# State-space gate of a hybrid attention and state-space block: two single passes of 512 columns against one paired pass of 1024 columns behind the state-space part

## The chip, the cores and the metric

The kernel runs on one core of a Trainium2 chip. The metric is device time in microseconds (us), median of several runs; lower is better. Names of engines are those of the profile: PE is TensorE's matmuls and PEld its weight loads, DVE is VectorE, ACT is ScalarE, POOL is GpSimd, and SP is SyncE, which issues nearly all DMAs.

## The reference

One layer: an RMS norm, one wide projection, dilated attention on one branch, a chunked state-space scan on the other, and two sigmoid gates that mix the branches. There are 256 rows (tokens), D is 2048, and the state-space width is 4096 in 8 groups. All data are fp32.

```python
hn = rms_norm(x, norm_w)
proj = hn @ w_in
q, k, v, z_a, z_s, xbc, dt_raw, g_a, g_s = jnp.split(proj, split_points, axis=-1)
...
y = rms_norm(y * jax.nn.silu(z_s), ssm_norm_w)
merged = jax.nn.sigmoid(g_a) * (o_a @ w_attn_branch) + jax.nn.sigmoid(g_s) * (y @ w_ssm_branch)
return x + merged @ w_out
```

The change concerns g_s, the gate of the state-space branch: 2048 columns, in quarters of 512 that the kernel numbers 0 to 3.

## The kernel before

**Products in three parts.** Each fp32 weight is split into a high part (h, an ACT copy, L276) and a low part (l, a DVE subtraction, L277). A product is then three matmuls: high by high, high by low, low by high. The weights come in units of 1024 columns (512 KB). A unit passes through three rings with a slot count each: w (5 slots, the load), h and l (4 slots each).

**Single pass.** `gates` (L588) calls `gemm_b` (L399): 16 steps of the inner dimension, two row blocks, three matmuls of 512 columns each, so 96 matmuls for one quarter of g_s. ACT then writes the tanh of the sums into th_s (L591).

**Paired pass.** `gemm_pair` (L461) makes 1024 columns at once. It walks over quads: two steps of the inner dimension by two row blocks by two column blocks. A plain quad is eight block products of three matmuls, 24 in all, out of two units. A quad listed in `S_QUADS` is done with seven block products (Strassen's scheme in Winograd's form), 21 matmuls. For these it loads wa and a sum of weight blocks wt, part of the fourth block wc, and sums of blocks of the left operand (sx). It makes ha and la from wa, hc and lc from wc (all four in the rings h and l, L550 and L552), then ht and lt from wt, and hu and lu from wa less wt (these in the pool `mul`). Where a (pass, quad) is listed in `presum`, the sum wt has been made ahead by DVE, sent to DRAM (`sum_jobs`, L242) and is loaded back (L525). Eight PSUM banks are used: four accumulators es and four products prods, one set on the tag g and the other on m1 and m2; `swap` says which. `fold` (L577) puts the products together. `room` gives places of their own for wt and wc ("wt", "wc") and for some of the ht and lt ("tl").

**Stages in order.** First come dt and quarters 0 and 1 of g_s; then eight groups of the state-space part, each with projections B, C and four pairs xs, zs (`project`, one bank of tag g each). Quarter 2 of g_s stands ahead of group 4 and quarter 3 behind group 7 (L947). Then follow paired passes for the state-space branch (ssm, L990), for v (L1023), the heads of attention, the gate g_a, the attention branch and the output.

**The tail of a group.** Work that waits for data is put off with `after(ticks, f)`; a tick is one projection or two units. For a group these are `turn` (transposes of xs, L793), four `decays` (L772: a load into acb, ACT operations into gt, a DVE product at the end of every second one), `scan` (L811, 32 small matmuls on PE, which read gt) and two `gather` (L828, DVE and ACT, which write yT). gt, acb, xdt and y1 have one buffer each. `tick(final=True)` (L948) puts out whatever is left.

**Places.** The tail's buffers lie in the pool `ssm` (L685), which closes after L948. The pools `mul` (L951), `xk` (L965) and `xp` (L977) are opened behind it and take the same part of the on-chip memory. Tiles of one tag share its slots. Within an engine, the order of instructions is fixed when the kernel is built: an instruction that comes earlier in the program has priority, one that isn't ready is overtaken, and the splits of units are lifted by 120 places (L274, L547).

The left sums sx of x for quads 2, 4, 5 and 6 are made in the group loop and kept in DRAM (`left_x`, L902); `fetch_left` (L429) brings one back: a POOL cast of one column behind a given unit, then a DMA on SP.

Of the kernel before, what the change touches and what calls it, by code (L numbers as in the profile page):

```python
# [1 line left out]

# [7 lines left out]
F32 = mybir.dt.float32  # L10
F32R = mybir.dt.float32r
# [24 lines left out]
N_ACT_X = 1  # L36
DT_LAG, CB_LAG, TURN_LAG, GT_LAG, Y_LAG, S_LAG, M_LAG = 2, 5, 3, 2, 11, 2, 2
Y_AFTER = 0, 0
GS_BEFORE = {0: (0, 1), 4: (2,)}
A_ORDERS = {0: (0, 1, 2, 4, 3, 6, 5, 7), 2: (0, 2, 1, 4, 3, 5, 6, 7)}  # L40
V_ORDERS = {0: (0, 2, 4, 1, 3, 5, 6, 7), 2: (0, 2, 1, 4, 3, 5, 6, 7)}
G_ORDERS = {c: (0, 2, 1, 4, 3, 5, 6, 7) for c in (0, 2)}
# [3 lines left out]
NEG = -1.0e30  # L46
S_QUADS = {
    ("ssm", 0): (5, 7, 8, 10, 11, 12, 13), ("ssm", 2): (3, 5, 7, 8, 10, 11, 12, 13),
    ("v", 0): (2, 3, 4, 5, 6), ("v", 2): (2, 4, 5, 6), ("ga", 0): (2, 4, 5, 6), ("ga", 2): (2, 4, 5, 6),
    ("attn", 0): (2, 4, 6), ("attn", 2): (2, 4, 5, 6), ("out", 0): (3, 5), ("out", 2): (3, 5),  # L50
}
# [7 lines left out]
SUMS_ATT = [(t, q) for t in [(n, c) for n in ("ga", "attn", "out") for c in (0, 2)] for q in S_QUADS[t]]  # L59
ATT_QUADS = sorted({*S_QUADS[("attn", 0)], *S_QUADS[("attn", 2)]})  # L60
IN_PLACE = {"ssm": [(0, 12), (2, 12)]}
SUMS_SSM = [(t, q) for t in (("ssm", 0), ("ssm", 2), ("v", 0), ("v", 2)) for q in S_QUADS[t] if (t[1], q) not in IN_PLACE.get(t[0], ())]
SUM_UNITS = 2, 9, 16
LEFT_EVERY, ATT_EVERY = 11, 4
SUM_LAG = 3
ROOM_SSM = 2
# [15 lines left out]
def weight_plan():  # L82
    plan = []

    def cols(tag, src, off, n_kt):
        plan.append((tag, "a", src, off, n_kt, P))

    def rows(tag, src, off, n_kt):
        plan.append((tag, "b", src, off, n_kt, 512))

    def pair(tag, src, off, n_kt):
        plan.append((tag, "p", src, off, n_kt, 1024))

    plan.append((("first", 0), "m", "w_in", (OFF_B, OFF_C, OFF_X, OFF_ZS), KT, 512))
    plan.append((("dt", 0), "a", "w_in", OFF_DT, KT, SH))
    for g in range(GROUPS):
        for c in GS_BEFORE.get(g, ()):
            rows(("gs", c), "w_in", OFF_GS + c * 512, KT)
        if g > 0:
            cols(("B", g), "w_in", OFF_B + g * P, KT)  # L100
            cols(("C", g), "w_in", OFF_C + g * P, KT)
        for t in range(max(4 * g, 1), 4 * g + 4):
            cols(("xs", t), "w_in", OFF_X + t * P, KT)
            cols(("zs", t), "w_in", OFF_ZS + t * P, KT)
    rows(("gs", 3), "w_in", OFF_GS + 3 * 512, KT)
    for c in (0, 2):
        pair(("ssm", c), "w_ssm_branch", c * 512, 2 * KT)
    for c in (0, 2):
        pair(("v", c), "w_in", OFF_V + c * 512, KT)
    for h in range(NH):  # L110
        cols(("q", h), "w_in", OFF_Q + h * P, KT)
        cols(("k", h), "w_in", OFF_K + h * P, KT)
        cols(("za", h), "w_in", OFF_ZA + h * P, KT)
    for c in (0, 2):
        pair(("ga", c), "w_in", OFF_GA + c * 512, KT)
    for c in (0, 2):
        pair(("attn", c), "w_attn_branch", c * 512, KT)
    for c in (0, 2):
        pair(("out", c), "w_out", c * 512, KT)
    return plan  # L120
# [76 lines left out]
def hybrid_block(ctx: ExitStack, tc: tile.TileContext, wall, xt, x, pk_d, cst_d, fw_d, out):  # L197
# [26 lines left out]
    def bank(tag, bufs, name):  # L224
        return ps.tile([P, 512], F32, name=name, tag=tag, bufs=bufs)
# [70 lines left out]
    def two_kts(t, q):  # L296
        t, q = (t[q // 4], q % 4) if isinstance(t, list) else (t, q)
        return t[:, 2 * q : 2 * q + 2, :]
# [130 lines left out]
    def fetch_left(kept, pool, bufs, key, x, spare, u):  # L429
        def get(behind):  # L430
            sx = new_sx(pool, bufs, spare, f"{key[0]}{key[1]}")
            gp.tensor_copy(sx[:, 0, 0, 0:1], behind)
            nc.sync.dma_start(sx.bitcast(F32), lefts[key])
            kept[key[1]] = left_parts(sx, x, spare)

        behind_unit(u, get)
# [151 lines left out]
    def gates(tag, th, src, scales=(0.5, 0.5)):  # L588
        accs = gemm_b(tag, lambda kt: kt_of(src, kt))
        for i in range(2):  # L590
            ac.activation(th[:, i, tag[1] * 512 : tag[1] * 512 + 512], accs[i], AF.Tanh, scale=scales[i])  # L591
# [93 lines left out]
    with tc.tile_pool(name="ssm", bufs=2) as sp:  # L685
# [223 lines left out]
        for g in range(GROUPS):  # L909
# [9 lines left out]
            for t in range(max(4 * g, 1), 4 * g + 4):  # L919
# [24 lines left out]
                zh = ev.tile([P, S], F32, name=f"zh{t}", tag="eh", bufs=2)  # L944
                evac(acc, zh, f"z{t}", scale=0.5)
                half_silu(zh, state["zs"][-1][:, i], f"z{t}")
        gates(("gs", 3), th_s, XT)  # L947
        tick(final=True)  # L948


    mul = ctx.enter_context(tc.tile_pool(name="mul", bufs=1))  # L951

    def scale_gate():
        tot = bank("m1", 2, "tot_y")
        for i in range(2):
            for n in range(2):
                pe.matmul(
                    tot[:, 2 * i : 2 * i + 2], ssq[:, n, i * P : (i + 1) * P], ones[:, 0:2],
                    start=(n == 0), stop=(n == 1),
                )  # L960
        _, hr = rsqrt_rows(tot[:, 0:4:2], INNER, "y")
        for i in range(2):
            ac.activation(th_s[:, i], th_s[:, i], AF.Identity, scale=hr[:, i : i + 1], bias=hr[:, i : i + 1])
# [1 line left out]
    xk = ctx.enter_context(tc.tile_pool(name="xk", bufs=1))  # L965
    sx_of_x = {}

    for n, q in enumerate(SX_X[:1]):
        fetch_left(sx_of_x, xk, 1, ("x", q), two_kts(XT, q), 0, plain_unit(("ssm", 2), 12, Y_ORDERS[2]))
    def room_of(t, n_wt, n_wc):  # L970
        t = t.rearrange("p (n m) -> p n m", m=512)
        return {
            "wt": [t[:, 2 * n : 2 * n + 2].rearrange("p n m -> p (n m)") for n in range(n_wt)],
            "wc": [t[:, 2 * n_wt + n] for n in range(n_wc)],
        }

    with tc.tile_pool(name="xp", bufs=1) as xp:  # L977
        sxs = {}
        ssm_room = room_of(xp.tile([P, ROOM_SSM * 512], F32, name="room_s", tag="room"), 0, ROOM_SSM)

        def left_y(q):
            spare = Y_SPARE[q]
            sx = new_sx(xp, sum(s == spare for s in Y_SPARE.values()), spare, f"y{q}")
            sxs[q] = turn_x(sx, ring(f"sxt_y{q}").rearrange("p (n m) -> p n m", n=2), two_kts(yT, q), spare)

        for q in SX_Y:
            if q in Y_LATE:
                continue
            fetch_left(sxs, xp, sum(s == Y_SPARE[q] for s in Y_SPARE.values()), ("y", q), two_kts(yT, q), Y_SPARE[q], plain_unit(("ssm", 0), Y_ORDERS[0].index(q) - 3 if q in S_QUADS[("ssm", 0)] else 12, Y_ORDERS[0]))
        for c in (0, 2):  # L990
            es, prods = gemm_pair(
                ("ssm", c), lambda kt: kt_of(yT, kt), 2 * KT, sxs, c == 2, {} if c else {2: [scale_gate], **{u: [lambda q=q: left_y(q)] for q, u in Y_LATE.items()}},
                1, Y_ORDERS[c], ssm_room,
            )
            tmp = [mul.tile([P, UNIT], F32, name=f"tmp_{t}{c}", tag=t, bufs=2) for t in ("ht", "lt")]
            dst = [t[:, n * 512 : n * 512 + 512] for t in tmp for n in range(2)]
            fold(prods, dst)
            for d, e, g in zip(dst, es, blocks(th_s, c)):
                ve.tensor_tensor(d, e, d, ALU.add)
                ve.tensor_tensor(g, g, d, ALU.mult)  # L1000
# [15 lines left out]
    with tc.tile_pool(name="vx", bufs=1) as vx:  # L1016
        tl = big.tile([P, 4, UNIT], F32R, name="tl_v", tag="yo0b")
        room["tl"] = [(tl[:, 2 * n], tl[:, 2 * n + 1]) for n in range(2)]
        for n, q in enumerate(SX_V):
            fetch_left(sx_of_x, vx, len(SX_V), ("x", q), two_kts(XT, q), 0, FIRST[("v", 0)])  # L1020
        for n, q in enumerate(SX_X[1:]):
            fetch_left(sx_of_x, xl, len(SX_X) - 1, ("x", q), two_kts(XT, q), 0, FIRST[("v", 0)] + 1 + n)
        for c in (0, 2):  # L1023
            es, prods = gemm_pair(
                ("v", c), lambda kt: XT[:, kt, :], KT, sx_of_x, c == 2, order=V_ORDERS[c], room=room
            )
            dst = blocks(vt, c)
            fold(prods, dst)
            for d, e in zip(dst, es):
                ve.tensor_tensor(d, e, d, ALU.add)  # L1030
    sx_of_o = {}

    with tc.tile_pool(name="att", bufs=2) as ap:
# [55 lines left out]
        for h in range(NH):  # L1089
            q, k = (ap.tile([P, S], F32, name=f"{n}T{h}", tag=f"{n}T", bufs=2) for n in "qk")  # L1090

            for n, d in (("q", q), ("k", k)):
                evac(project((n, h)), d, f"{n}{h}")
            p = ap.tile([P, 384], F32, name=f"p{h}", tag="p", bufs=2)
            pT = ap.tile([P, 384], F32, name=f"pT{h}", tag="pT", bufs=1)
            za = ap.tile([P, S], F32, name=f"za{h}", tag="za", bufs=3)
            after(S_LAG + (6, 4, 2)[max(h - 13, 0)], lambda a=(h, pT, za): mix(*a))
            after(S_LAG + (3 if h < 15 else 1), lambda a=(h, p, pT): turn_p(*a))
            after(S_LAG + (h == 0), lambda a=(h, q, k, p): scores(*a))
            zh = ev.tile([P, S], F32, name=f"zah{h}", tag="eh", bufs=2)  # L1100
            evac(project(("za", h)), zh, f"za{h}", scale=0.5)
            half_silu(zh, za, f"za{h}")
# [169 lines left out]
```

## Time and profile before

| what | value |
|---|---|
| median of 3 runs | 1385.69 us (1385.48 to 1386.45) |
| profiled execution, span from first to last instruction | 1383.8 us |
| mean granted TensorE clock | 0.998 |
| group loop up to the last projection | about 80 to 558 us |
| last single gate pass (quarter 3) | 558 to 581 us |
| scan of group 7 on PE | 581 to 584 us |
| paired passes of the state-space branch | 584 to 748 us |
| DMA moved | 345 MB, mean 249 GB/s |

The span is that of one profiled execution, 1.9 us below the median of the runs. Times in the views are counted from the start of that span. In the view of windows the columns are: the window, its length, busy time of PE, PEld, DVE, ACT and POOL (with the number of instructions), the granted clock, the DMA share and GB/s. In the view of waits a line reads: who waited, for whom, us in total, times, the longest. In the timeline: start, duration, engine, line, operation, what it writes and reads, how many were merged.

### The profile page before, as it was taken

The numbers are of one execution on the slowest core, as the hardware profiler recorded it, in microseconds if no ns is written. First come the engines' busy times: TensorE is split into PE (matmuls) and PEld (weight loads), VectorE is DVE, ScalarE is ACT, GpSimd is POOL, SyncE is SP. The second block draws the span as 40 slices with busy tenths as digits, with TensorE's granted clock in tenths as the row PEclk, the third lists the DMA queues.
The fourth block names the chain that finished last, engine by engine and source line by source line (L and its number), as shares of the span: only waits on it lengthen the run. The fifth ranks groups of instructions, "written<-read, shape, count | busy, mean of one in ns | idle before, by whom it ended". The sixth has DMA issues, their size and how long they took to land.

```text
span 1383.8 us, 20696 instructions
## 1 busy us (share of the span) xinstructions
PE 1373.6 (99%) x7266; PEld 1169.9 (85%) x7266; DVE 1169.5 (85%) x1753; ACT 835.5 (60%) x1306; POOL 142.0 (10%) x226
## 2 busy tenths in 40 slices
PE   9999999999999999999999999999999999999997
PEld 8888888888888888888888888888888888888886
DVE  7898999987799898789889897777877788888897
ACT  7656677675667675766565554544544556655564
POOL 2301111101011100010001001111111000000112
PEclk9999999999999999999999999999999999999999
DMA  9767988868787866668677668888888757865773
GB/s 347 231 187 225 313 254 291 279 224 287 245 266 240 294 212 208 188 224 280 230 259 267 222 209 278 275 275 273 299 288 301 241 161 264 294 222 180 243 273 122
DMA packets 105080, 345.00 MB, mean 249 GB/s; under 512 B 11728, under 2 KB 13712, under 8 KB 104976
## 3 DMA queue, kind: packets, MB, share of 16 engines
q1 hardware_dynamic: 103536, 339.62, 74.0%
q10 hardware_dynamic: 1440, 4.06, 0.8%
q8 instruction: 57, 0.93, 0.3%
q14 instruction: 47, 0.39, 0.1%
HBM read 314.87 MB, written 28.77 MB: 248 GB/s over the span
## 4 chain that ended last, share of the span: by engine, by line
PE 97%; DMA 1%; DVE 1%; ACT 1%; issue 0%; SPq 0%; POOL 0%; POOLq 0%; DVEq 0%; ACTq 0%
PE ps_zs L329 8%; PE ps_xs L329 8%; PE ps_zs L332 4%; PE ps_q L329 4%; PE ps_za L329 4%; PE ps_k L329 4%; PE ps_xs L332 4%; PE ps_ssm L476 3%; PE ps_ssm L477 3%; PE ps_ssm L478 3%; PE ps_q L332 2%; PE ps_k L332 2%; PE ps_za L332 2%; PE ps_gs L414 2%; PE ps_gs L412 2%; PE ps_gs L413 2%
## 5 line engine op out<-in xcount | busy, mean ns | idle before, releaser
L276 ACT ACTIVATE h<-w 128x1024 fp32r<-128x1024 f32 (+1 forms) x398 | 413.9, 1047 | 318.0 <-issue 78.8
L277 DVE TENSOR_TENSOR l<-w,h 128x1024 fp32r<-128x1024 f32 (+1 forms) x398 | 479.4, 1211 | 124.2 <-ACT h L276 121.8
L329 PE MATMUL ps_zs<-XT,h 128*128 128x512 f32 x496 | 176.3, 397 | 0.0
L329 PE MATMUL ps_xs<-XT,h 128*128 128x512 f32 x496 | 175.9, 396 | 0.0
L332 PE MATMUL ps_zs<-XT,l 128*128 128x256 f32 x496 | 139.9, 282 | 0.0
L332 PE MATMUL ps_xs<-XT,l 128*128 128x256 f32 x496 | 139.8, 282 | 0.0
L329 PEld LDWEIGHTS ps_xs<-XT,h 128*128 128x128 f32 x496 | 93.3, 188 | 21.7
L329 PEld LDWEIGHTS ps_zs<-XT,h 128*128 128x128 f32 x496 | 93.4, 188 | 21.2
L332 PEld LDWEIGHTS ps_zs<-XT,l 128*128 128x128 f32 x496 | 93.7, 189 | 1.5 <-issue 0.7
L332 PEld LDWEIGHTS ps_xs<-XT,l 128*128 128x128 f32 x496 | 93.7, 189 | 0.4
L329 PE MATMUL ps_q<-XT,h 128*128 128x512 f32 x256 | 92.5, 405 | 0.2 <-ACT h L276 0.2
L329 PE MATMUL ps_k<-XT,h 128*128 128x512 f32 x256 | 89.9, 395 | 0.0
L329 PE MATMUL ps_za<-XT,h 128*128 128x512 f32 x256 | 89.7, 394 | 0.0
L543 ACT ACTIVATE ha<-wa 128x1024 fp32r<-128x1024 f32 x43 | 45.4, 1055 | 46.4 <-DMA wa<-in_wall 10.9
L332 PE MATMUL ps_q<-XT,l 128*128 128x256 f32 x256 | 71.2, 278 | 0.0
L332 PE MATMUL ps_k<-XT,l 128*128 128x256 f32 x256 | 71.1, 278 | 0.0
L332 PE MATMUL ps_za<-XT,l 128*128 128x256 f32 x256 | 71.1, 278 | 0.0
L544 DVE TENSOR_TENSOR la<-wa,ha 128x1024 fp32r<-128x1024 f32 x43 | 52.5, 1220 | 11.9 <-ACT ha L543 11.8
L782 ACT ACTIVATE gt<-acb,acT 128x128 f32<-128x128 f32 x128 | 44.2, 391 | 23.7 <-DMA acb<-acum_d 21.9
L329 PEld LDWEIGHTS ps_q<-XT,h 128*128 128x128 f32 x256 | 48.2, 188 | 11.5 <-ACT h L276 0.6
L329 PEld LDWEIGHTS ps_za<-XT,h 128*128 128x128 f32 x256 | 48.1, 188 | 11.3
L329 PEld LDWEIGHTS ps_k<-XT,h 128*128 128x128 f32 x256 | 48.1, 188 | 11.2
(688 smaller groups left out, 3325.1 us busy)
## 6 DMA issues: line engine op xcount, KB each, us to landing
w<-in_wall SPq DMA_DIRECT2D x394, 512.0 KB, 4.7
wa<-in_wall SPq DMA_DIRECT2D x43, 512.0 KB, 4.9
th_a<-in_wall SPq DMA_DIRECT2D x19, 512.0 KB, 5.6
sums_at<-in_wall SPq DMA_DIRECT2D x18, 512.0 KB, 4.7
acb<-acum_d SPq DMA_DIRECT2D x32, 256.0 KB, 4.0
t_ssm<-sums_at SPq DMA_DIRECT2D x13, 512.0 KB, 4.1
wt<-t_ssm SPq DMA_DIRECT2D x13, 512.0 KB, 5.4
th_a<-in_wall SPq DMA_DIRECT2D x19, 256.0 KB, 6.0
```

What stands on the lines that cost most here:

```text
L276: ac.activation(h[:, a:b], w[:, a:b], AF.Copy)
L277: ve.tensor_tensor(l[:, a:b], w[:, a:b], h[:, a:b].bitcast(F32), ALU.subtract)
L329: pe.matmul(acc, h[:, kk, :], m, start=(kt == 0), stop=False)
L332: pe.matmul(acc[:, S:], l[:, kk, :], m[:, :S], start=False, stop=(kt == KT - 1))
L412: pe.matmul(accs[i], xh, h[:, kk], start=(kt == 0), stop=False)
L413: pe.matmul(accs[i], xh, l[:, kk], start=False, stop=False)
L476: pe.matmul(acc, xh, h, start=start, stop=False)
L477: pe.matmul(acc, xh, l, start=False, stop=False)
L478: pe.matmul(acc, xl, h, start=False, stop=stop)
L543: ac.activation(h, src, AF.Copy)
L544: ve.tensor_tensor(l, src, h.bitcast(F32), ALU.subtract)
L782: ac.activation(g4[:, n, b], acb[:, j, b // 2 * P : b // 2 * P + P], AF.Relu, scale=-1.0, bias=sc[:, h : h + 1],)
```

## The change

Quarters 2 and 3 of g_s are made in one paired pass, ("gs", 2), which comes behind the closed pool ssm and ahead of the state-space branch. Its order is quads 0, 1, 2, 4, 3, 5, 6, 7, and quads 2, 4, 5 and 6 have seven products. It has a pool of its own, gx: places for two wt and one wc, one pair of ht and lt more, and three sx; the sx of quad 2 goes to xk and is kept for the pass v. Four weight sums are added to those made ahead, and these are now made four times in a group instead of three: 24 of them instead of 18. With one paired pass more in front, the passes ssm and v exchange their sets of banks, the sum of squares tot_y moves from tag m1 to g, and q and k of head 0 go to m1 and m2.

```diff
-GS_BEFORE = {0: (0, 1), 4: (2,)}
+GS_BEFORE = {0: (0, 1)}
+GS_ORDER = (0, 1, 2, 4, 3, 5, 6, 7)
...
+    ("gs", 2): (2, 4, 5, 6),
...
-SUMS_SSM = [(t, q) for t in (("ssm", 0), ("ssm", 2), ("v", 0), ("v", 2)) for q in S_QUADS[t] if (t[1], q) not in IN_PLACE.get(t[0], ())]
-SUM_UNITS = 2, 9, 16
+SUMS_SSM = [(t, q) for t in (("gs", 2), ("ssm", 0), ("ssm", 2), ("v", 0), ("v", 2)) for q in S_QUADS[t] if (t[1], q) not in IN_PLACE.get(t[0], ())]
+SUM_UNITS = 1, 6, 11, 16
...
-    rows(("gs", 3), "w_in", OFF_GS + 3 * 512, KT)
+    pair(("gs", 2), "w_in", OFF_GS + 2 * 512, KT)
...
-        gates(("gs", 3), th_s, XT)
         tick(final=True)
...
-        tot = bank("m1", 2, "tot_y")
+        tot = bank("g", 4, "tot_y")
...
-    for n, q in enumerate(SX_X[:1]):
-        fetch_left(sx_of_x, xk, 1, ("x", q), two_kts(XT, q), 0, plain_unit(("ssm", 2), 12, Y_ORDERS[2]))
...
+    with tc.tile_pool(name="gx", bufs=1) as gx:
+        room = room_of(gx.tile([P, 5 * 512], F32, name="room_g", tag="room"), 2, 1)
+        tl = gx.tile([P, 2, UNIT], F32R, name="tl_g", tag="tl")
+        room["tl"] = [(tl[:, 0], tl[:, 1])]
+        sx_of_g = {}
+        for n, q in enumerate(SX_X):
+            pool, kept = (gx, sx_of_g) if n else (xk, sx_of_x)
+            fetch_left(kept, pool, max(n and len(SX_X) - 1, 1), ("x", q), two_kts(XT, q), 0, FIRST[("gs", 2)] + n)
+        es, prods = gemm_pair(
+            ("gs", 2), lambda kt: XT[:, kt, :], KT, ChainMap(sx_of_g, sx_of_x), False, order=GS_ORDER, room=room
+        )
+        dst = blocks(th_s, 2)
+        fold(prods, dst)
+        for d, e in zip(dst, es):
+            ve.tensor_tensor(d, e, d, ALU.add)
+            ac.activation(d, d, AF.Tanh, scale=0.5)
...
-                ("ssm", c), lambda kt: kt_of(yT, kt), 2 * KT, sxs, c == 2, {} if c else {2: [scale_gate], **{u: [lambda q=q: left_y(q)] for q, u in Y_LATE.items()}},
+                ("ssm", c), lambda kt: kt_of(yT, kt), 2 * KT, sxs, c == 0, {} if c else {2: [scale_gate], **{u: [lambda q=q: left_y(q)] for q, u in Y_LATE.items()}},
...
-                ("v", c), lambda kt: XT[:, kt, :], KT, sx_of_x, c == 2, order=V_ORDERS[c], room=room
+                ("v", c), lambda kt: XT[:, kt, :], KT, sx_of_x, c == 0, order=V_ORDERS[c], room=room
...
-                evac(project((n, h)), d, f"{n}{h}")
+                evac(project((n, h), None if h else {"q": "m1", "k": "m2"}[n]), d, f"{n}{h}")
```

More of the change, by code (lines that the diff above doesn't have):

```diff
@@ L1 @@
+from collections import ChainMap
 from contextlib import ExitStack, nullcontext
```

## The prediction, made before the changed kernel ran

> **What bounds the kernel now.** I read the page first, then who PE waits for, then busy time by stage.
>
> ```profile
> span 1383.8 us, 20696 instructions
> ...
> PE 1373.6 (99%) x7266; PEld 1169.9 (85%) x7266; DVE 1169.5 (85%) x1753; ACT 835.5 (60%) x1306; POOL 142.0 (10%) x226
> ...
> PEclk9999999999999999999999999999999999999999
> ```
> ```profile
> PE ps_q L329 <- ACT h L276: 0.2, 1, 0.2
> ```
> ```profile
> 80.00:293.00 213.00, 213.00 (x1273) 184.41 (x1272) 194.85 (x336) 143.86 (x270) 25.85 (x54) 1.00 0.82 265
> ...
> 316.00:558.00 242.00, 242.00 (x1452) 209.32 (x1451) 207.56 (x337) 159.90 (x299) 22.27 (x48) 1.00 0.76 247
> 558.00:580.70 22.70, 22.70 (x106) 18.72 (x104) 17.78 (x20) 17.32 (x34) 0.00 (x0) 1.00 0.64 196
> ```
>
> TensorE sets the time: it is busy 99% of the span at the full clock, and its one wait after the start is 0.2 us. In the windows (PE, PEld, DVE, ACT, POOL, clock, DMA share, GB/s) PE fills the group loop and also the last gate pass (558 to 580.7). So a matmul taken away is worth its spacing, but only while PE never runs dry; in this kernel any hole in PE is paid in full. The question is whether the pass in its new place can keep PE fed.
>
> **The change: what it removes.** These rows of PE's timeline carry the sum (start, duration):
>
> ```profile
> 549.78 2.82 PE L820 MATMUL yp<-gt,xdt 128*64 128x256 f32 x32
> ...
> 557.93 0.28 PE L332 MATMUL ps_zs<-XT,l 128*128 128x256 f32 x1
> ...
> 558.74 0.39 PE L412 MATMUL ps_gs<-h,XT 128*128 128x512 f32 x1
> ...
> 561.46 0.39 PE L412 MATMUL ps_gs<-h,XT 128*128 128x512 f32 x1
> ...
> 564.18 1.03 PE L801 MATMUL xtp<-cst,xs 128*128 128x128 f32 x8
> 564.97 0.47 PE L412 MATMUL ps_gs<-h,XT 128*128 128x512 f32 x1
> ```
> ```profile
> 580.83 2.82 PE L820 MATMUL yp<-gt,xdt 128*64 128x256 f32 x32
> 583.58 0.50 PE L476 MATMUL ps_ssm<-h,yTa 128*128 128x512 f32 x1
> ```
>
> From 558.74 to 561.46 twelve 512-column matmuls start: 2.72/12 = 0.227 us each. Two single passes are 2 x 96 = 192 of them; the new pass has four plain quads of 24 and four of 21, 180. **Saved: 12 x 0.227 = 2.7 us**, 0.2% of the time.
>
> **What it moves.** The last projection ends at Z (here 558.05, after the 557.93 row; earlier by one gate pass afterwards). Behind Z stands the tail of the last group: decays, transposes, scan, gather. Now that tail lies beside the third gate pass and four plain quads of the ssm pass. Afterwards no gate pass stands there, and only two plain quads come before the first quad of seven products. That quad needs the pools mul, xk and gx, which are opened where the closed pool ssm lay. The waits of SP and ACT from 583 to 600, before:
>
> ```profile
> SPq L526 <- DVE yT L288: 3.8, 1, 3.8
> ```
> ```profile
> ACT htt L543 <- DVE yT L288: 2.0, 1, 2.0
> ```
> ```profile
> 583.70 0.88 DVE L833 SCALAR_TENSOR_TENSOR y<-xs,pk,yp 128x256 f32<-128x256 f32 x2 [0.45 <-PE yp L820]
> ...
> 588.31 1.22 DVE L277 TENSOR_TENSOR l<-w,h 128x1024 fp32r<-128x1024 f32 x1
> ...
> 593.24 0.48 DVE L288 SCALAR_TENSOR_TENSOR yT<-y,pk,yT 128x256 fp32r<-128x256 f32 x1
> ```
>
> A load into room_s and a write of htt use none of yT, yet both wait for the last instruction on a tile of pool ssm (L288, end 593.72). I read this as: nothing of a new pool is touched before the whole old pool is free. Call that moment T; before, it is Z+35.7. It cost nothing there, since PE had the gate pass and plain quads.
>
> **When is T afterwards?** The chain, before:
>
> ```profile
> 554.65 0.33 SPq L777 DMA_DIRECT2D acb<-acum_d  x1
> ...
> 559.55 0.33 SPq L777 DMA_DIRECT2D acb<-acum_d  x1
> ...
> 566.05 0.33 SPq L777 DMA_DIRECT2D acb<-acum_d  x1
> ```
> ```profile
> 569.78 0.69 ACT L782 ACTIVATE gt<-acb,acT 128x128 f32<-128x128 f32 x2 [1.39 <-DMA acb<-acum_d]
> ```
> ```profile
> 573.77 1.75 DVE L791 TENSOR_TENSOR gt<-gt,cb 128x1536 f32<-128x1536 f32 x1
> ```
>
> The buffer gt is single and free after the scan before (549.78 + 2.8). Three more loads into the single acb follow one by one, each up to 3.7 us to landing (566.05 to 569.78) and then 1.8 of ACT; the last exponential and the 1.75 us of L791 close it. So gt is ready at 575.5 = Z+17.5; the scan then ran only at 580.83, because it stood behind the gate pass. Afterwards it runs when ready: Z+17 (one ACT split less in the way; bounds 15 and 17.5). Scan 2.75 us, then the gather: 583.70 to 593.72 = 10 us before, of which some 3 us were other DVE work such as 588.31; I take 8.5 (bounds 7 and 10). **T = Z+28.3** (bounds Z+25, Z+33; the upper with a scan at half clock).
>
> **What PE has until then.** 48 matmuls of two plain quads 10.9 us, transposes 0.8 (564.18 to 564.97), and the six products of quad 2's own ha, 1.4: PE is dry at Z+13.0, with the scan (2.75) to come. Plain quads 3 and 7 don't help if ring tiles h and l go out in program order: hc of quad 2 stands before them, and its source wc is in gx. The load of wt, which waits for T, heads SP's queue: behind it stand the w loads of quad 3 and on, of which the ring holds at most five, and nobody but the splits waits for them. On POOL the casts ahead of the sx loads wait too, and nothing that PE needs before T stands behind them. In the trace hc of quad 5 in ssm (604.85, in the fences below) goes ahead of the next plain quad's h (606.32), as the program has them, but nothing there forces the question.
>
> **When PE starts again.** Loads into new places, issue to landing, and the first product after T before:
>
> ```profile
> wt<-t_ssm SPq DMA_DIRECT2D x13, 512.0 KB, 5.4
> ...
> room_s<-in_wall SPq DMA_DIRECT2D x13, 256.0 KB, 4.1
> ...
> sx_x<-sxd_x SPq DMA_DIRECT2D x5, 512.0 KB, 4.9
> ```
> ```profile
> 601.89 0.39 PE L476 MATMUL pp_ssm<-htt,sx_y 128*128 128x512 f32 x1
> ```
> ```profile
> 604.85 0.61 ACT L543 ACTIVATE hc<-room_s 128x512 fp32r<-128x512 f32 x1
> ...
> 606.32 1.04 ACT L276 ACTIVATE h<-w 128x1024 fp32r<-128x1024 f32 x1
> ```
> ```profile
> L543 ACT ACTIVATE ha<-wa 128x1024 fp32r<-128x1024 f32 x43 | 45.4, 1055 | 46.4 <-DMA wa<-in_wall 10.9
> ...
> L544 DVE TENSOR_TENSOR la<-wa,ha 128x1024 fp32r<-128x1024 f32 x43 | 52.5, 1220 | 11.9 <-ACT ha L543 11.8
> ```
>
> sx is third in SP's queue: 1 + 4.9, so T+6 (bounds T+5, wc alone with hc; T+8.2, as 601.89 shows, where PE had other work). PE idles from Z+13.0 to Z+34.3 less the scan: **18.5 us**. Then 126 matmuls remain (28.6 us). Until the next wc has come through its one seat (4.1 + 1.3 us), DVE owes PE about ten operations of 1.22; I add 1.5 us (bounds 0 and 5).
>
> **The clock after the hole.** Windows at the end, PE's timeline at the start:
>
> ```profile
> 1374.00:1376.00 2.00, 1.50 (x13) 1.30 (x11) 1.82 (x6) 1.76 (x5) 0.36 (x2) 1.00 0.22 82
> ...
> 1380.00:1382.00 2.00, 0.00 (x0) 0.00 (x0) 0.00 (x0) 0.00 (x0) 0.00 (x0) 0.50 1.02 361
> ```
> ```profile
> 1.44 3.78 PE L623 MATMUL warm<-ssq 128*128 128x256 f32 x8 [1.44 <-DVE ssq L620]
> 4.66 2.27 PE L377 MATMUL ps_first<-yTa,h 128*128 128x512 f32 x4
> ...
> 7.47 0.86 PE L377 MATMUL ps_first<-yTa,h 128*128 128x512 f32 x3
> ```
>
> Five us after the last matmul the granted clock is 0.50. At the start PE is slow from 1.44 to about 6.7 (four matmuls take 2.27 us; three take 0.86 later): 5.3 us at half speed lose 2.6. (The page's PEclk row shows none of that; the spacing does.) A hole of 14 us should do the same: I add 2.3 us (bounds 0, if the lag falls under DVE's, and 2.9). The Trainium skill's page TensorE: Matmul & The Clock Gate (Part 1: The HAM clock gate) speaks against this change: about 3.4 us idle halve the clock, and as long a busy stretch restores it. By the page alone the term would be an estimated 1.7 us and the forecast 0.6 lower; the trace agrees on the half clock, and its 5.3 us is longer.
>
> **What costs nothing.** (1) Four quads of seven on DVE instead of single passes: per quad three splits and t2's subtraction, 1.22 each, and lc 0.7, 5.6 against 2.4 plain; in the dry stretch DVE is free, behind T it is the 1.5 above. (2) Presums: 24 jobs instead of 18, six times two DVE operations of 0.7 = 8 us, inside 80 to 558, where DVE is idle 18 + 34 us; uncovered, +8 at most. They save two sums in v. (3) More transfers (three sx again; with the presums some 25 more on SP at 0.33 each): the DMA share is 0.64 to 0.82. (4) The swapped banks and tot_y: each pass starts on banks that the last fold empties, under quad 7. (5) The pass gone from ahead of group 4: group 3's scan is due 11 ticks behind instead of 15, and the four ticks between were that pass's own. The 0.2 us wait at q may go or double; with the issue lost around it I allow 0.6 either way.
>
> **Sum.** -2.7 + 18.5 + 1.5 + 2.3 = +19.6. On the profiled execution: 1383.8 + 19.6 = 1403.4; the median of the runs is 1.9 above that span, which I keep: **1405.3 us**. Lowest terms: (25 + 5 - 15.8) - 2.7 - 0.6 = +10.9, 1396.6; highest: (33 + 8.2 - 15.8) + 5 + 2.9 - 2.7 + 0.6 = +31.2, 1416.9. Its own range, all ends not falling together: 1398 to 1414.
>
> **Rivals.** (a) *Faster or level*: the new pass stays hidden. Decided by T: if the places of mul, xk and gx are free by about Z+8, loads and splits (5 us) end at Z+13 and nothing is dry: 1385.7 - 2.7 = 1383.0, on the edge between faster and same. For it: PE has not idled at any hand-over so far. Against it: two engines that waited for L288, and a chain that no edit shortens by 20 us. (b) *Partly hidden*: PE gets quads 3 and 7 and quad 4's ha ahead of hc, 12.2 us more. The hole shrinks to 6.3; behind T four quads remain (16.3 us) that go at the pace of one wc seat (three times 6 us), +2.5; the fold then has no quad 7 over it, +1.9; clock 2.3: +10.3, 1396. For it: in the ssm pass plain matmuls overtake those of seven. (c) Presums or splits overload DVE beside the hole: up to 8 more, within the highest terms or just above.
>
> **How the numbers follow.** Forecast 0.78, (a) 0.12, (b) 0.08, worse than the highest terms 0.02. Range 1394 to 1414: the forecast's own and (b). 0.2% is 2.8 us, about what the measurement tells from no change. Of (a) half falls on each side of 1382.9: faster 0.06, same 0.06; slower 0.88.
>
> **What would show it.** Right: PE dry twice after the last zs, about 4 us before the last scan and 14 behind it; the second ends about 6 us after the last L288; SP and ACT wait for L288; 180 ps_gs and pp_gs matmuls; a half-clock stretch. Wrong: h of quad 3 written before hc of quad 2 (b); a write to gx, htt or sx_x before the last L288 (a); PE full through the pass.

## The result, and the profile after

| | before | after |
|---|---|---|
| median of the runs, us | 1386.07 (1385.48 to 1386.52, 4 runs) | 1408.97 (1407.7 to 1409.33, 4 runs) |
| profiled execution, span | 1383.8 | 1407.5 |
| mean granted TensorE clock | 0.998 | 0.993 |

The ratio is 1.0165, with a 95% interval of 1.0151 to 1.018: slower by 22.9 us. The forecast was 1405.3, in a range of 1394 to 1414. First the page after, with the chain's shares by engine as its last line:

```profile
span 1407.5 us, 20855 instructions
...
PE 1376.8 (98%) x7254; PEld 1168.6 (83%) x7254; DVE 1186.4 (84%) x1781; ACT 843.7 (60%) x1316; POOL 155.6 (11%) x247
...
PEclk9999999999999999899999999999999999999999
...
PE 86%; DVE 5%; DMA 5%; ACT 2%; issue 2%; SPq 0%; POOL 0%; POOLq 0%; DVEq 0%; ACTq 0%
```

PE's busy time rose by 3 us although it has fewer matmuls, because some ran at half clock (0.70 granted in the third window below); the rest of the 23.7 us is PE with nothing to do. Lines of the changed file stand three below those of before: L823 is the scan, L794 closes gt, L291 ends a gather, L546 and L547 split, L436 and L435 are the loads of left sums and the casts ahead of them, L528 and L529 load wt and wc. PE's four longest waits:

```profile
PE pp_gs L479 <- ACT ha L546: 9.2, 1, 9.2
PE yp L823 <- DVE gt L794: 3.6, 1, 3.6
PE ps_xs L335 <- DVE l L280: 1.9, 2, 1.6
PE ps_zs L332 <- ACT h L279: 1.6, 1, 1.6
```

Two waits stand behind Z, the end of the last projection. The next two stand ahead of it, and there the forecast had none. The windows of PE (columns as before) show both places:

```profile
80.00:541.30 461.30, 456.87 (x2732) 394.29 (x2731) 414.15 (x703) 311.99 (x593) 60.53 (x120) 1.00 0.79 270
541.30:553.10 11.80, 11.80 (x58) 9.66 (x56) 7.92 (x12) 8.05 (x22) 0.00 (x0) 1.00 0.43 135
553.10:582.00 28.90, 13.57 (x55) 8.55 (x54) 13.73 (x19) 9.96 (x17) 0.55 (x4) 0.70 0.40 150
582.00:608.00 26.00, 25.76 (x111) 20.26 (x110) 24.21 (x25) 16.77 (x20) 0.00 (x0) 1.00 0.66 216
```

Z is 541.30. With the gate pass gone from the loop (96 matmuls, 21.8 us) it should have been 558.05 - 21.8 = 536.25: **the group loop lost 5.05 us.** Behind Z the span has 1407.5 - 541.3 = 866.2 us, against 825.75 + 21.8 = 847.5 before, that pass added: 18.7 more. With 2.7 saved by twelve matmuls, **21.4 us were lost behind Z**, all in the third window: of its 28.9 us the scan (2.8) and the 21 products of quad 2 (4.8) are worth 7.6 at full clock.

The chain of waits of after goes through that window in these steps (start, duration):

```profile
548.51 3.70 DMA acb<-acum_d
...
555.08 1.77 DVE gt L794
556.89 4.52 PE yp L823 x32
...
568.61 0.49 DVE yT L291
569.30 0.56 POOL sx_x L435 x4
...
571.82 8.11 DMA room_g<-in_wall
580.01 0.64 ACT hc L546
```

The last load of acb, gt, the scan, the gather to 569.09 (T = Z+27.8), the casts on POOL, and then 8.1 us until wc has landed. SP's queue says why so long:

```profile
569.24 0.33 SPq L528 DMA_DIRECT2D room_g<-t_gs  x1
569.67 2.11 SPq L436 DMA_DIRECT2D sx_x<-sxd_x  x4
571.82 0.45 SPq L529 DMA_DIRECT2D room_g<-in_wall  x1
```

Four left sums, 2 MB, are issued ahead of wc; three of them belong to later quads.

### The profile page after: what moved, and what is told of

It reads as the page before. It is cut to its first block, busy times and chain, and to the rows that moved or that the text cites. A ratio compares the mean times of both kernels' runs of the same rounds, so it can differ in the third digit from the quotient of the medians.

```text
span 1407.5 us, 20855 instructions
## 1 busy us (share of the span) xinstructions
PE 1376.8 (98%) x7254; PEld 1168.6 (83%) x7254; DVE 1186.4 (84%) x1781; ACT 843.7 (60%) x1316; POOL 155.6 (11%) x247
## 4 chain that ended last, share of the span: by engine, by line
PE 86%; DVE 5%; DMA 5%; ACT 2%; issue 2%; SPq 0%; POOL 0%; POOLq 0%; DVEq 0%; ACTq 0%
PE ps_xs L332 6%; PE ps_zs L332 6%; PE ps_q L332 4%; PE ps_k L332 4%; PE ps_za L332 4%; PE ps_xs L335 3%; PE ps_zs L335 3%; PE ps_ssm L480 3%; PE ps_ssm L479 3%; PE ps_ssm L481 3%; PE ps_q L335 2%; PE ps_k L335 2%; PE ps_za L335 2%; PE ps_out L479 2%; PE ps_out L480 2%
## 5 line engine op out<-in xcount | busy, mean ns | idle before, releaser
L279 ACT ACTIVATE h<-w 128x1024 fp32r<-128x1024 f32 (+1 forms) x390 | 404.9, 1047 | 286.2 <-issue 67.6
L280 DVE TENSOR_TENSOR l<-w,h 128x1024 fp32r<-128x1024 f32 (+1 forms) x390 | 469.8, 1211 | 101.3 <-ACT h L279 99.4
L546 ACT ACTIVATE ha<-wa 128x1024 fp32r<-128x1024 f32 x47 | 49.6, 1054 | 36.8 <-PE ps_ssm L481 9.1
L547 DVE TENSOR_TENSOR la<-wa,ha 128x1024 fp32r<-128x1024 f32 x47 | 57.4, 1221 | 9.2 <-ACT ha L546 8.2
L547 DVE TENSOR_TENSOR ltu<-wa,htu 128x1024 fp32r<-128x1024 f32 x41 | 50.1, 1221 | 9.9 <-ACT htu L546 9.9
```

The source lines that it names most:

```text
L279: ac.activation(h[:, a:b], w[:, a:b], AF.Copy)
L280: ve.tensor_tensor(l[:, a:b], w[:, a:b], h[:, a:b].bitcast(F32), ALU.subtract)
L546: ac.activation(h, src, AF.Copy)
L547: ve.tensor_tensor(l, src, h.bitcast(F32), ALU.subtract)
```

## The experiments

Where two versions differ by a microsecond or two, the medians carry it only in part (ranges of 2 to 4 us), so two marks of the profiled execution are compared as well: Z, which shows the group loop, and the span behind Z, which shows the pass and all after it. Each mark is from one execution: those of e3 and e4 are the fastest of their four, 2.4 and 2.9 us below the median, and that of e1 is the slowest, 2.3 above. T is the end of the last instruction on the old pool.

| run | median, us | Z | span less Z | T | PE's first product behind T |
|---|---|---|---|---|---|
| before | 1386.1 | 558.05 | 825.75 | Z+35.7 | (never dry) |
| after | 1409.0 | 541.30 | 866.2 | Z+27.8 | T+1.5, dense from T+12.9 |
| e1 sums_18 | 1408.8 | 536.85 | 872.3 | | |
| e2 plain_pass | 1391.2 | 540.48 | 846.9 | | (never dry) |
| e3 casts_away | 1406.8 | 540.84 | 861.7 | Z+25.4 | T+6.7 |
| e4 plain_third | 1405.5 | 539.84 | 861.0 | Z+25.7 | T+1.6 |
| e5 lag_4 | 1406.9 | 537.97 | 867.8 | | |
| e6 casts_third | 1404.2 | 540.90 | 861.6 | Z+29.2 | T+7.0 |
| e7 late_T | 1414.2 | 541.10 | 871.1 | Z+32.8 | T+1.6 |
| e8 two_unmade | 1392.8 | 536.49 | 853.9 | Z+37.9 | |
| e9 third_behind | 1400.4 | 540.76 | 857.5 | Z+25.8 | T+6.8 |
| e10 two_behind | 1385.8 | 536.46 | 847.5 | Z+30.5 | (waits 1.2 and 0.7) |
| e11 before_sums | 1390.2 | 562.03 | 825.3 | | (never dry) |

**e1: sums at three units again.**

```diff
-SUM_UNITS = 1, 6, 11, 16
+SUM_UNITS = 2, 9, 16
```

> Weight sums made three times in a group again (18 in all instead of 24), all else as in the changed kernel (1409.0). Theory A, the denser sums cost the 5 us that the group loop lost: DVE keeps a fixed order and stands at the subtraction of a sum until its load has landed, and splits behind it come late. With 18 at the old units these waits go back to what before had: PE is full from 80 us to the last projection, which ends near 536.5 instead of 541.3, and the time is 1403.5 to 1405.5. Rival B, the gate pass that is gone from ahead of group 4 costs it (group 3's tail now lies beside projections): the last projection still ends at 540.5 to 541.5 and the time is 1408 to 1410.

The time stayed at 1408.82 (1408.28 to 1411.14), and yet theory A holds for the loop. Windows of e1, the loop and the pass v up to q's first product, and below them the same of v after:

```profile
80.00:536.85 456.85, 456.85 (x2734) 394.79 (x2733) 411.78 (x691) 312.41 (x593) 48.63 (x102) 1.00 0.76 255
768.70:850.40 81.70, 79.99 (x337) 63.38 (x335) 74.46 (x82) 44.35 (x51) 2.56 (x3) 0.98 0.56 191
```

```profile
773.00:850.40 77.40, 77.40 (x343) 64.12 (x342) 68.99 (x72) 45.00 (x51) 4.03 (x3) 1.00 0.66 227
```

PE is full in the loop and Z is back at 536.85. The gain is lost again in v, which with the four sums of the new pass ahead of it in the list keeps one sum of the five it had: DVE makes the rest there, and 337 matmuls take 81.7 us, where 343 take 77.4 after (before: 337 in 76.5). The 24 sums are a trade: they cost 5 us in the loop and save about that in v.

**e2: eight plain quads in the new place.**

```diff
-    ("gs", 2): (2, 4, 5, 6),
+    ("gs", 2): (),
...
-        fold(prods, dst)
         for d, e in zip(dst, es):
-            ve.tensor_tensor(d, e, d, ALU.add)
-            ac.activation(d, d, AF.Tanh, scale=0.5)
+            ac.activation(d, e, AF.Tanh, scale=0.5)
```

> The paired pass stays behind the state-space part, but all its eight quads are plain: nothing of it needs a place of a new pool, no left sums are brought back for it (that of quad 2 is for v and comes later, as before), 192 matmuls instead of 180. 22 sums are asked for, in the same 24 places. Theory A, the hole is the wait for new places (and for what stands behind it): PE runs through, 43.6 us of plain quads against a T near Z+28; of the 21.3 us lost behind Z all go, 2.7 come back as matmuls, the group loop's 5 us stay: 1388 to 1393. Rival B, the hole comes from the scan and gather now lying behind the pass's head, whatever the quads are: PE still idles over 8 us ahead of the scan or behind it and the time is 1400 or more.

1391.19 (1389.17 to 1393.56). The window of the whole pass, scan included:

```profile
540.48:587.80 47.32, 47.32 (x234) 38.72 (x233) 32.18 (x39) 29.35 (x50) 0.00 (x0) 1.00 0.64 199
```

No hole, full clock. So neither the new place nor the tail beside it makes the hole; the seven-product quads with their new places do. What remains against before, 5.1 us, is for the most part the loop: Z is 4.2 late.

**e3: left sums without the casts.** A DMA at the head of each quad that uses its sum.

```diff
-            fetch_left(kept, pool, max(n and len(SX_X) - 1, 1), ("x", q), two_kts(XT, q), 0, FIRST[("gs", 2)] + n)
+            extra[q] = [lambda n=n, q=q, pool=pool, kept=kept: fetch_now(kept, pool, max(n and len(SX_X) - 1, 1), ("x", q), two_kts(XT, q))]
...
+    def fetch_now(kept, pool, bufs, key, x):
+        sx = new_sx(pool, bufs, 0, f"{key[0]}{key[1]}")
+        nc.sync.dma_start(sx.bitcast(F32), lefts[key])
+        kept[key[1]] = left_parts(sx, x, 0)
```

> The four left sums are no longer brought back by a POOL cast behind units 0 to 3 with a DMA ahead of wc, but by the DMA alone, issued at the head of the quad that uses them. Theory A: (1) the casts read a column of h of units 0 to 3, and while POOL waits for T they hold all four slots of the ring h, so ha of quad 2 could not be written before T; without them it is, and PE has six more products, 1.4 us, before the scan; (2) three left sums, 1.5 MB, no longer stand ahead of wc, so hc of quad 2 comes at about T+6 instead of T+10.9. Together 5 to 6.5 us less: 1402.5 to 1404.5. Rival B, the lag behind T is set by the bytes that all loads move together or by DVE and not by the order: ha may come early, hc stays at T+9 or later, 1407 to 1409.5.

ACT of after, and then ACT and PE of e3 (whose lines stand five lower):

```profile
569.52 1.06 ACT L546 ACTIVATE ha<-wa 128x1024 fp32r<-128x1024 f32 x1 [1.15 <-POOL sx_x L435]
```

```profile
549.42 1.06 ACT L551 ACTIVATE ha<-wa 128x1024 fp32r<-128x1024 f32 x1 [1.52 <-PE ps_gs L486]
```

```profile
553.78 0.39 PE L486 MATMUL ps_gs<-ha,XT 128*128 128x512 f32 x1
555.74 2.82 PE L828 MATMUL yp<-gt,xdt 128*64 128x256 f32 x32 [1.57 <-DVE gt L799]
572.86 1.22 PE L484 MATMUL pp_gs<-htt,sx_x 128*128 128x512 f32 x2 [14.30 <-ACT htt L551]
```

Both halves of theory A are in the trace. In after, ha waited for POOL's casts, though its wa had been issued 40 us before, at 529.5: each cast reads a column of h of one of units 0 to 3, POOL stood at the first until T, and so all four slots of the ring h stayed taken. In e3 ha comes 20 us earlier; PE is dry at Z+13.2, waits 1.57 us instead of 3.62, and the scan runs at full clock. And hc of quad 2 is written at T+6.6 (572.83) instead of T+10.9 (580.01). Behind Z this is worth 4.5 us, a little under the 5 to 6.5 expected; the medians show only 2.2 (1406.77, of 1404.36 to 1408.72), which lies above A's range and just under B's. It is the trace that tells A from B.

**e4: quad 3 third.**

```diff
-GS_ORDER = (0, 1, 2, 4, 3, 5, 6, 7)
+GS_ORDER = (0, 1, 3, 2, 4, 5, 6, 7)
```

> Quad 3 (plain) goes ahead of quad 2 (seven products): order 0, 1, 3, 2, 4, 5, 6, 7. Theory A, the casts hold the four slots of h until T: the third plain quad cannot be split before T, PE is dry at about Z+11.8 as with the changed kernel, but its 24 matmuls (5.4 us) then fill the lag behind T in which PE waited for hc: first matmul at T+2, time 1403.5 to 1405.5. Rival B, nothing holds h: PE is dry only at Z+17, h of quad 3 is written before the scan, and the time falls by the same 5.4 us or a little more (1402.5 to 1404). Rival C, the lag behind T only moves: 1408 to 1409.5. The trace, not the time, tells A from B.

```profile
551.42 0.39 PE L481 MATMUL ps_gs<-h,XT 128*128 128x512 f32 x1
555.00 2.82 PE L823 MATMUL yp<-gt,xdt 128*64 128x256 f32 x32 [3.19 <-DVE gt L794]
567.07 2.07 PE L479 MATMUL ps_gs<-h,XT 128*128 128x512 f32 x4 [9.24 <-ACT h L279]
```

1405.53 (1402.59 to 1406.83), 5.2 us less behind Z, and it is A: PE is dry at Z+11.8 as in after, a third plain quad notwithstanding, and h of quad 3 is written only behind T. The quad helps by filling the lag behind T. Not all of the 5.2 is the quad's: the scan ran at full clock (2.82 us against 4.50 after), which no theory had, and T came 2.1 us earlier, mostly for it. The median fell by 3.4.

**e5: subtractions one unit later.**

```diff
-SUM_LAG = 3
+SUM_LAG = 4
```

> Still 24 weight sums, but DVE's two subtractions of each are put four units behind the one that starts the load, not three. Theory A, the group loop loses its 5 us because DVE, in its fixed order, stands at the first subtraction until the load has landed (17.5 us in 8 waits, the longest 4.0, against 0.2 before): one unit later, about 2.7 us, takes most of these waits away; they fall under 7 us, the last projection ends at 537 to 539 and the time is 1404.5 to 1407. Rival B, it is the work of six more sums (8 us of DVE, six more loads and stores) wherever it stands: the last projection ends at 540 or later and the time is 1408 to 1410. Rival C, the next load, now one unit behind the subtraction and in the same buffer, is late in its place: no gain or worse.

The row that names the cause, of before, after, and e5, in the loop:

```profile
DVE sums_at L252 <- DMA sums_at<-in_wall: 0.2, 1, 0.2
```

```profile
DVE sums_at L255 <- DMA sums_at<-in_wall: 17.5, 8, 4.0
```

```profile
DVE sums_at L255 <- DMA sums_at<-in_wall: 10.2, 8, 2.5
```

1406.92 (1405.66 to 1408.31); Z at 537.97 instead of 541.30 with the same 24 sums. So the work of the sums is hidden, as predicted; their place in DVE's order is not. DVE stands at the subtraction until the load has landed, the splits behind it are late, and PE waits for them. One such wait of after, ACT, DVE and PE:

```profile
211.58 1.06 ACT L279 ACTIVATE h<-w 128x1024 fp32r<-128x1024 f32 x1 [2.29 <-DMA w<-in_wall]
```

```profile
214.14 0.69 DVE L255 TENSOR_TENSOR sums_at<-sums_at 128x512 f32<-128x512 f32 x1 [3.99 <-DMA sums_at<-in_wall]
214.75 0.42 DVE L400 SCALAR_TENSOR_TENSOR ct<-th_C,cv_C 128x256 f32<-128x256 f32 x1
...
216.69 1.22 DVE L280 TENSOR_TENSOR l<-w,h 128x1024 fp32r<-128x1024 f32 x1
```

```profile
215.22 0.70 PE L771 MATMUL cbp<-ct,bt 128*128 128x256 f32 x2 [0.80 <-DVE ct L400]
```

The h of the unit is there at 212.64; its l, behind the subtraction, comes 4 us later, and PE waits for ct, which stands behind it too. The Trainium skill, PSUM — Partial Sum Buffer (section Engine vs sequencer instructions), has the queues of ScalarE, VectorE and GpSimdE as strict FIFO; these rows of DVE agree. The rest of the waits, 10.2 us, was more than the 7 expected; whether they or the work of the sums make the 1.1 us by which Z is still behind e1 is open. The medians fell by 2.1 only: behind Z e5 is 1.6 longer, 0.9 of it a slower scan (last section).

**e6: e3 and e4 together.**

> Both edits together: left sums fetched by a DMA alone at the head of their quad, and the order 0, 1, 3, 2, 4, 5, 6, 7. Theory A, the casts had held the ring h: now the third plain quad is split and multiplied before T, PE is dry only some 5.4 us later than with the casts away alone (the last matmul before the long hole at about Z+21 with the scan among them), T stays at Z+25.5 and the restart at T+6.6, so the hole shrinks by 5.4: 1399.5 to 1402.5. Rival B, something else holds h or w until T (the queue of SP, the order of ACT): h of quad 3 is written after the last gather and the time is that of e4 or of e3, 1404 to 1407.

1404.22 (1404.04 to 1405.12): 2.5 below e3 by the medians, and nothing behind Z (861.6 against 861.7). The third quad was indeed done before T; the gain did not come. PE and DVE of e6:

```profile
559.61 2.82 PE L828 MATMUL yp<-gt,xdt 128*64 128x256 f32 x32
577.02 1.22 PE L484 MATMUL pp_gs<-htt,sx_x 128*128 128x512 f32 x2 [14.59 <-ACT htt L551]
```

```profile
554.90 1.23 DVE L552 TENSOR_TENSOR la<-wa,ha 128x1024 fp32r<-128x1024 f32 x1 [1.95 <-ACT ha L551]
556.04 1.75 DVE L799 TENSOR_TENSOR gt<-gt,cb 128x1536 f32<-128x1536 f32 x1
```

The scan has no wait any more, since it stands behind the cover: it starts at Z+18.7 instead of Z+14.9. T moved with it, from Z+25.4 to Z+29.2, and the hole with T (14.59 us against 14.30). The part of e6's expectation that kept T at Z+25.5 was wrong.

**e7: T four us later.**

```diff
+                if u == 15:
+                    for _ in range(6):
+                        ve.tensor_tensor(y1, y1, zs, ALU.mult)
```

> Six more DVE products of y1 by zs (0.69 us each, in place, read by nobody) behind the last gather of the last group: the old pool ssm comes free about 3.7 to 4.1 us later, nothing else changes. Theory A, the restart of PE hangs on the whole old pool being free: SP's load of wt, POOL's casts and ha all move by the same 4 us, and so does the time: 1412.5 to 1413.5 (behind Z the trace is 3.7 to 4.1 us longer). Rival B, the restart hangs on yT or on the loads that were under way: PE starts at the same time, 1408 to 1410.

```profile
569.58 4.33 DVE L849 TENSOR_TENSOR y<-y,zs 128x512 f32<-128x512 f32 x6
```

```profile
574.21 0.55 POOL L435 CAST sx_x<-h 128x1 fp32r<-128x1 f32 x4 [56.03 <-DVE y L849]
```

1414.18 (1413.44 to 1418.52): 5.2 us more by the medians, 4.9 behind Z, for 4.33 us of products that nobody reads; the scan ran wholly at half clock (5.39 us against 4.50), which is the rest. POOL waited for these products, which have nothing to do with left sums, and so did SP with the load of wt, which goes to another place of another new pool:

```profile
SPq L528 <- DVE y L849: 25.4, 1, 25.4
```

So it is not one tile's place that counts; I read it as the whole old pool.

**e8: two quads of seven, sums not made ahead.** The edit also takes the casts away (as e3, with the DMA behind the quad's splits), drops the places for wt and wc, and takes the new pass out of SUMS_SSM, which leaves the 18 sums of before.

```diff
-    ("gs", 2): (2, 4, 5, 6),
+    ("gs", 2): (5, 6),
...
-GS_ORDER = (0, 1, 2, 4, 3, 5, 6, 7)
+GS_ORDER = (0, 1, 2, 3, 4, 5, 6, 7)
...
-SUM_UNITS = 1, 6, 11, 16
+SUM_UNITS = 2, 9, 16
```

> The pass behind the state-space part with what the runs so far say it can carry: seven products for quads 5 and 6 alone, behind five plain quads (order 0 to 7); their weight sums are not made ahead (18 sums at the old units, as before the change), wa and wb come through the ring w before T; left sums fetched by a DMA alone at the head of the products, two instead of four. Theory A: PE has 27.2 us of plain quads, 0.8 of transposes, 2.75 of scan and 1.4 of ha before it is dry, at about Z+32, and T+5 is Z+31 to Z+32: no hole or one below 2 us, group loop full, v as before; six matmuls less are worth 1.4 us: 1384 to 1386.5, same as before within what can be measured. Rival B, DVE (two subtractions more in each of these quads) or the one queue of SP makes a hole of 4 us or more: 1388 to 1392.

1392.75 (1392.19 to 1393.28): just above rival B's range, and for another reason. PE's waits behind Z come to 5.5 us. PE and DVE of e8:

```profile
558.59 2.82 PE L829 MATMUL yp<-gt,xdt 128*64 128x256 f32 x32
```

```profile
561.46 0.87 DVE L842 SCALAR_TENSOR_TENSOR y<-xs,pk,yp 128x256 f32<-128x256 f32 x2 [1.33 <-PE yp L829]
...
573.47 0.87 DVE L291 SCALAR_TENSOR_TENSOR yT<-y,pk,yT 128x256 fp32r<-128x256 f32 x2
```

The loop is full (Z 536.49). But the scan stands at Z+22.1 behind plain quads, and the gather, 7.7 us in after, takes 12.9 among splits: T at Z+37.9. That this order, and not DVE's extra work, makes the waits is tested in e10.

**e9: e6 with the order pinned.** Unit 7 is the second half of quad 3.

```diff
+                if n == FIRST[("gs", 2)] + 7:
+                    stay_behind("gt_act", insts[0])
+                    stay_behind("gt", insts[1])
...
+                    keep = (lambda i: stay_behind("scan", i)) if (tag[0], q) == ("gs", 3) and j > 3 else lambda i: i
```

> As e6 (casts away, quad 3 third), but the second half of quad 3 (its split of unit 7 on ACT and DVE, its 12 matmuls on PE) is pinned behind the last exponential, the last L791 product and the last scan matmul; nothing is added or taken away. e6 had 5.4 us more cover than e3 and the same time. Theory A: the cover was given back because T slid: e6's third quad stood ahead of gt's last steps on ACT and DVE and of the scan on PE (scan at Z+18.8, T at Z+29.2; in e3 Z+15.0 and Z+25.5). Pinned, the scan is back at Z+15 to Z+16, T at Z+26, half of the quad lies between scan and restart: the long hole shrinks by 4 to 5 us and the time is 1399 to 1401. Rival B, the restart hangs on loads or on DVE and not on T: no change, 1403.5 to 1405.

```profile
556.10 2.82 PE L844 MATMUL yp<-gt,xdt 128*64 128x256 f32 x32 [0.65 <-DVE gt L813]
...
573.34 1.22 PE L496 MATMUL pp_gs<-htt,sx_x 128*128 128x512 f32 x2 [10.09 <-ACT htt L564]
```

1400.4 (1398.88 to 1401.46). Same work as e6; the scan is back at Z+15.3, T at Z+25.8, and the hole 4.5 us shorter, as the sliding T says.

**e10: e8 with the order pinned.** As in e9 with unit 5 and quad 2, and the first subtraction of each quad of seven behind the last gather.

> As e8 (two quads of seven, sums not made ahead), with the same pinning: second half of the third quad (quad 2) behind the last exponential, the last L791 product and the scan, and the first subtraction of quad 5's sum behind the last gather. Theory A: e8's scan stood at Z+22.1 behind plain quads and its gather took 13 us among splits, so T came at Z+37.9; now scan near Z+15.5, gather with three or four splits ahead of it and one among it, T at Z+28 to Z+31, and PE, with plain quads and ha until Z+33, waits 2 to 4 us for sx (T+5): 1387 to 1390. Rival B, T does not matter there, the wait is DVE's two more subtractions a quad: 1392 to 1393.5.

1385.83 (1384.34 to 1386.82, 10 runs), ratio to before 1.0001 (0.9991 to 1.001). Better than expected: all of PE's waits of the execution but the start's are

```profile
PE yp L848 <- DVE gt L817: 1.2, 1, 1.2
...
PE ps_gs L497 <- ACT h L287: 0.7, 1, 0.7
```

T came at Z+30.5, and rival B is out: the two extra subtractions are there and the hole is gone. The six matmuls less (1.4 us) about pay for these two waits.

**e11: the kernel before with denser sums.**

```diff
-SUM_UNITS = 2, 9, 16
+SUM_UNITS = 1, 6, 11, 16
```

> The kernel before with one edit: weight sums at four units in a group instead of three (22 jobs asked for, all made, instead of 18). The gate pass stays ahead of group 4 and behind group 7. Theory A, the denser sums alone make the group loop's loss (DVE standing at the first subtraction for its load): the last projection ends 3 to 5 us later than in before (561 to 563 instead of 558.05), and v, with nine sums made instead of five, gives back 0 to 1: 1388.5 to 1391. Rival B, the sums only hurt together with the moved gate pass, without which there is slack in every group: 1385 to 1387.

1390.19 (1389.11 to 1390.67), ratio 1.0032 (1.002 to 1.0044). Z moved by 4.0 us to 562.03 with the gate passes where they always were, and behind Z nothing but 0.4 us came back. The wait of DVE is there too:

```profile
DVE sums_at L252 <- DMA sums_at<-in_wall: 12.1, 6, 4.6
```

## Why the prediction was right, and where it was off

| term, us | forecast | measured |
|---|---|---|
| twelve matmuls less | -2.7 | -2.7 |
| PE dry, DVE behind, half clock | 18.5 + 1.5 + 2.3 = 22.3 | 21.4 |
| group loop and the rest | 0 | +5.0 |
| sum on the profiled executions | +19.6 | +23.7 |

- **The bound and the mechanism** held: a hole in PE is paid in full, and nothing of a new pool is touched before the old one is free. e2 (no new places: no hole) and e7 (T later: as much later) show it; that each tile waits for the whole old pool is the simplest reading of them, not a separate test. Rival (a), hidden, needed T at about Z+8; rival (b) needed quads 3 and 7 to overtake hc, and h of quad 3 was written at 585.08, behind even hc of quad 4 (584.54).
- **The sum behind Z** is nearer than its terms, which is luck. In the third window PE stood for 28.90 - 13.57 = 15.3 us, where the first two terms have 20.0; its matmuls there, worth 7.6 us, took 13.6 at a granted clock of 0.70, so 6.0 more, where the clock term has 2.3.
- **T** was Z+28.3 in the forecast and Z+27.8 in the trace, in part by luck: gt was ready 1.5 us sooner (556.84, Z+15.5) and the gather 0.85 shorter, and the scan at half clock, which the forecast had only in its upper bound, gave 1.8 back.
- **The dry point** was early: Z+11.8 and not Z+13.0. "Nothing that PE needs before T stands behind them", said of POOL's casts, was wrong: no instruction stood behind them, but the h slots that they read did, and ha of quad 2 could not be written. e3 and e4 show it.
- **The restart** at T+6 was mis-sized both ways. The first product came at T+1.5, PE was dense only at T+12.9. "sx is third in SP's queue" did not count the sx of the later quads: all four went ahead of wc. With them out of the way (e3) wc's product comes at T+7.7 and PE starts at T+6.7 and stays full.
- **"What costs nothing", (2)**, is the step that failed: the sums were priced as 8 us of DVE work inside 52 us of idle time, and as work they are hidden. Not counted was that DVE waits in its fixed order for each sum's load, which three units behind was not there in 8 of 24 cases when the sums were five units apart. That cost 5.0 us (e1: gone with 18 sums; e5: mostly gone with the subtraction later; e11: there without the rest of the change). Rival (c) had up to 8 us for it, though by overload. "They save two sums in v" no run separates: with four more of them e11 gained 0.4 us behind Z, with four fewer than before e1 lost 5 in v.
- **(5)**, the moved gate pass, cost nothing: e1 has it and a full loop. The small wait at q went.

The two errors, 0.9 us too much behind Z and 5.0 too little ahead of it, leave the measured median 3.7 us above the forecast.

Open: why these loads come late is not shown. Those of 512 KB took a median of 6.3 us from issue to landing after, 4.7 before and 4.5 in e1, but no run separates what slows them. In e11 only 1.8 us of the loop's 4.0 show as idle time of PE, the rest lies in slightly longer spacings. Not tried: a second buffer for the sums' loads, places outside the old pool, and a shift of e10's pin by some matmuls, worth at most its 1.2 us wait, less than a measurement can tell.

## What to carry to other kernels

Ask of a buffer what has to be finished before its place is free, and price the time from there, not from when its data could be loaded; a helper instruction that touches the new place, such as a one-column cast, holds whatever it reads until then. Cover put in front of a chain can push the chain back by as much as it covers: check where the chain's own instructions then stand on each engine (e6 against e9, e8 against e10, 4 to 7 us for order alone). Work of an in-order engine that waits for a DMA is priced by the wait at its place in the order, and an engine's idle share says nothing of that.

## What the runs showed of the hardware

A pause of a little over 3 us ahead of the scan decides over its clock here. The scan of e4 and that of e5, the same 32 matmuls:

```profile
555.00 2.82 PE L823 MATMUL yp<-gt,xdt 128*64 128x256 f32 x32 [3.19 <-DVE gt L794]
```

```profile
553.19 5.38 PE L823 MATMUL yp<-gt,xdt 128*64 128x256 f32 x32 [3.25 <-DVE gt L794]
```

After 3.19 us of waiting they ran at full speed (granted clock 1.00 over the scan), after 3.25 at half speed throughout (0.50), and after 3.39 (e7) likewise. But after 3.53 (e1) and 3.62 (after) the scan took 4.50 us at 0.62, so the slow part ended sooner: the length of the pause alone does not settle it. The Trainium skill, TensorE: Matmul & The Clock Gate (Part 1: The HAM clock gate), gives an idle window of about 3.4 us, with a phase that runs freely; these waits lie within about 0.2 us of it on both sides. Whether the length or the phase parted e4 from e5, two runs do not tell. Either way the scan's clock is worth up to 2.6 us here, and T moves with it.
